# Half-filled experts added in pairs, the last sum read back early: a two-layer decoder trunk

## The chip, the cores and the metric

One core of a Trainium2 chip runs the whole program. The metric is the device time of one execution in microseconds (us). PE is TensorE, DVE is VectorE, ACT is ScalarE, POOL is GpSimd, and SP is SyncE, which issues nearly all weight transfers.

## The reference

512 tokens of width 1024 pass two layers. Each layer has a mixer and a mixture of experts, each shifted and scaled by six vectors that a product with `c` gives (adaLN), each followed by a layer norm.

```python
for layer in range(2):
    mod = silu(c) @ ada_w[layer] + ada_b[layer]
    sh1, sc1, g1, sh2, sc2, g2 = split(mod, 6)
    h = x * (1 + sc1) + sh1
    y = moba_gla_mixer(h, ...) if layer == 0 else gated_deltanet_mixer(h, ...)
    x = layer_norm(ALPHA * x + g1 * y)
    h = x * (1 + sc2) + sh2
    y = shared_expert(h) + sum over the token's 6 of 64 experts of
        weight * ((silu(h @ w_gate[e]) * (h @ w_up[e])) @ w_down[e])
    x = layer_norm(ALPHA * x + g2 * y)
```

All of it is float32. An expert has 3 MB of weights (gate and up 1024 x 256 each, down 256 x 1024).

## The kernel before

**Stages.** From 0 to 75 us the first modulation is made: eight slabs of `ada_w`, multiplied and summed by DVE (L256), turned by PE (L1743), applied to x in `start` (L1744 to L1751), and then the first projection starts. Layer 0's mixer runs to about 335 us, the routing to 402 us, its expert loop to 1028 us, layer 1's mixer and routing to 1496 us, and its expert loop to 2117 us; a tail with the last layer norm ends the program.

**Experts.** The experts are sorted by how many tokens chose them. The 20 fullest have a block of 128 slots of their own (called alone here), 28 share a block by two (twos, 14 blocks, 64 slots each), 16 by four (fours, 4 blocks, 32 slots each): 38 blocks for a layer, `BLOCKS`. The order in which the blocks run is made by `spread`. By experts in a block it is `11112121412121214121212121412121214122`.

**One turn of the loop** (`moe`, written out by hand, so the order on PE is that of the code). Turn b gathers the tokens of a later block (`xg`, an indirect DMA of POOL), turns them (`turn`, L1324), multiplies block b by gate and up (`widen`, L1336; ACT and DVE make `hh`), turns that back (`turn_back`, L1347), and multiplies block b-1 by down (`narrow`, L1369). A block of four has two experts at a time, so its `narrow` comes in two halves. What an alone block gives is added to a DRAM tensor `acc` by an indirect DMA of POOL (L1376). What a shared block gives is split in a high and a low part (`yh`, `yl`, L1383 to L1385) and goes to its tokens by matmuls with a 0/1 matrix (`combine`, L1396): for each of 8 tiles of 128 x 512 two matmuls, then one DVE add into x (L1397). The shared expert's down projection (`shared_end`, L1440) lies in turns 8 to 22.

**Weights.** SP issues them in order. Gate and up have five slots, down has a ring of three: the down weights of an expert can be issued when those of the third expert before have been used, and whatever stands behind them on SP waits too.

**End of the loop.** In the last turn POOL reads `acc` back in 8 pieces of 128 x 512 (L1615) and DVE adds them to x (L1616). Then all engines meet at a branch (`extra`, L1690, experts that outgrew their block: none here), the last block is added by L1396/L1397, and DVE does the layer norm (statistics L312 and L314, application L321 and L322; for x[0] in the last tail ACT and POOL, L329 to L331).

## Time and profile before

| | us |
|---|---|
| median of 3 runs (lowest to highest) | 2151.9 (2149.96 to 2156.48) |
| the profiled execution, its own time | 2150.13 |
| its span from first to last instruction | 2148.1 |
| PE busy | 1955.6 (91%) |
| DVE busy | 1236.2 (58%) |
| ACT busy | 508.3 (24%) |
| POOL busy | 441.2 (21%) |
| DMA queue of SP's transfers, share of 16 engines | 60.1% |

The shares are means over stages that differ: in the expert loops, 1247 of the 2148 us, PE and the DMA engines are both above nine tenths, elsewhere the DMA engines are far below.

### The profile page before, as it was taken

How to read it: one execution, taken by the hardware profiler on the slowest of the kernel's cores; microseconds unless marked ns; L12 is line 12 of the kernel's file. 1: busy time of each engine (PE TensorE's matmuls, PEld its weight loads, DVE VectorE, ACT ScalarE, POOL GpSimd, SP SyncE). 2: the span in 40 equal slices, each digit the busy share in tenths (PEclk: the TensorE clock that was granted, in tenths of full speed). 3: DMA queues.
4: the chain of work that ended last, by engine and by line, in shares of the span. 5: the costliest groups of instructions: out<-in, count | busy, mean ns of one | idle time of the engine just before them, and what ended most of it. 6: DMA issues, size and time to landing. Idle time of an engine off the chain costs nothing. (4 is left out here: it accounts for less than half of the span.)

```text
span 2148.1 us, 28655 instructions
## 1 busy us (share of the span) xinstructions
PE 1955.6 (91%) x10619; PEld 1193.5 (56%) x10619; DVE 1236.2 (58%) x3169; ACT 508.3 (24%) x969; POOL 441.2 (21%) x313
## 2 busy tenths in 40 slices
...
GB/s 296 257 240 186 182 199 195 352 330 325 406 349 351 389 316 361 381 325 300 96 118 59 40 60 60 46 99 309 357 335 365 363 327 402 353 317 405 329 348 126
DMA packets 128679, 572.18 MB, mean 266 GB/s; under 512 B 16943, under 2 KB 54255, under 8 KB 72473
## 3 DMA queue, kind: packets, MB, share of 16 engines
q1 hardware_dynamic: 103600, 499.81, 60.1%
...
q14 instruction: 58, 0.47, 0.1%
...
## 5 line engine op out<-in xcount | busy, mean ns | idle before, releaser
L1336 PE MATMUL ps_mm<-wslot,xT 128*64 128x512 f32 (+2 forms) x1216 | 404.5, 596 | 1.1 <-ACT xT L1325 0.8
L1369 PE MATMUL ps_mm<-wslot,hT 128*64 128x512 f32 (+2 forms) x1024 | 329.6, 627 | 20.1 <-DMA wslot<-in_moe_w_down_dram 19.9
L1338 DVE SCALAR_TENSOR_TENSOR hh<-hh,t,ps_mm 128x256 f32<-128x256 f32 x76 | 36.5, 480 | 434.5 <-ACT hh L1337 434.5
L1336 PE MATMUL ps_mm<-parts,xT 128*64 128x512 f32 (+2 forms) x832 | 280.0, 595 | 0.7 <-ACT xT L1325 0.4
L1336 PEld LDWEIGHTS ps_mm<-wslot,xT 128*64 128x64 f32 (+2 forms) x1216 | 142.1, 148 | 218.9 <-issue 205.7
L1369 PEld LDWEIGHTS ps_mm<-wslot,hT 128*64 128x64 f32 (+2 forms) x1024 | 105.5, 152 | 225.1 <-issue 197.5
L232 PE MATMUL ps_mm<-parts,hTh 128*128 128x256 f32 x704 | 206.7, 295 | 14.0 <-DVE op L400 6.9
L1294 POOL DMA_INDIRECT xg<-hd,idx x76 | 86.3, 1136 | 615.1 <-PE ps_tr L1396 525.4
L233 PE MATMUL ps_mm<-parts,hTh 128*128 128x256 f32 x704 | 204.0, 291 | 4.9 <-DVE parts L220 4.2
L234 PE MATMUL ps_mm<-parts,hTl 128*128 128x256 f32 x704 | 203.3, 291 | 0.0
L225 POOL TENSOR_TENSOR parts<-wslot,parts 128x512 fp32r<-128x512 f32 (+1 forms) x79 | 140.6, 1807 | 241.9 <-ACT parts L218 241.8
L1397 DVE TENSOR_TENSOR x<-x,ps_tr 128x512 f32<-128x512 f32 x288 | 183.6, 680 | 11.1 <-PE ps_tr L1396 10.4
L1337 ACT ACTIVATE hh<-ps_mm 128x256 f32<-128x256 f32 x76 | 29.2, 384 | 613.7 <-PE ps_mm L1336 613.7
L1376 POOL DMA_INDIRECT acc<-yh,row x40 | 64.8, 1620 | 498.9 <-DVE yh L1375 498.9
L1336 PEld LDWEIGHTS ps_mm<-parts,xT 128*64 128x64 f32 (+2 forms) x832 | 93.7, 144 | 130.5 <-issue 122.9
L1396 PE MATMUL ps_tr<-yh,ohs 128*128 128x512 f32 x288 | 137.4, 477 | 26.1 <-DVEq L1690 14.0
L232 PEld LDWEIGHTS ps_mm<-parts,hTh 128*128 128x128 f32 x704 | 137.3, 195 | 17.7 <-DVE op L400 4.6
L1325 ACT ACTIVATE xT<-ps_tr 128x512 f32<-128x512 f32 x152 | 84.0, 597 | 245.0 <-PE ps_tr L1324 245.0
L233 PEld LDWEIGHTS ps_mm<-parts,hTh 128*128 128x128 f32 x704 | 137.4, 195 | 6.8 <-DVE parts L220 4.8
L234 PEld LDWEIGHTS ps_mm<-parts,hTl 128*128 128x128 f32 x704 | 136.8, 195 | 2.2 <-issue 0.9
L234 PE MATMUL ps_mm<-hTh,parts 128*128 128x512 f32 (+1 forms) x296 | 120.6, 407 | 9.1 <-POOL parts L225 9.1
L232 PE MATMUL ps_mm<-hTh,parts 128*128 128x512 f32 (+1 forms) x296 | 123.7, 418 | 5.1 <-ACT parts L218 2.5
...
## 6 DMA issues: line engine op xcount, KB each, us to landing
wslot<-in_moe_w_down_dram SPq DMA_DIRECT2D x128, 1024.0 KB, 10.4
wslot<-in_moe_w_gate_dram SPq DMA_DIRECT2D x76, 1024.0 KB, 8.2
wslot<-in_moe_w_up_dram SPq DMA_DIRECT2D x76, 1024.0 KB, 11.7
parts<-in_moe_w_gate_dram SPq DMA_DIRECT2D x52, 1024.0 KB, 10.3
parts<-in_moe_w_up_dram SPq DMA_DIRECT2D x52, 1024.0 KB, 8.8
wslot<-in_ada_w_dram SPq DMA_DIRECT2D x44, 1024.0 KB, 5.6
wslot<-in_od_w_in_dram SPq DMA_DIRECT2D x16, 1024.0 KB, 6.2
wslot<-in_ev_w_in_dram SPq DMA_DIRECT2D x12, 1024.0 KB, 6.4
```

Of the source, the lines that this page charges most:

```text
L225: eng.tensor_sub(lo[:, ks], v[:, ks], hi[:, ks].bitcast(F32))
L232: self.nc.tensor.matmul(out, ah, bh, start=(i == 0), stop=False)
L233: self.nc.tensor.matmul(out, ah, bl, start=False, stop=False)
L234: self.nc.tensor.matmul(out, al, bh, start=False, stop=(i == n - 1))
L1294: self.nc.gpsimd.indirect_dma_start(out=xg, out_offset=None, in_=M["hd"], in_offset=bass.IndirectOffsetOnAxis(ap=idx, axis=0), bounds_chec ...
L1325: nc.scalar.activation(xT[:, 4 * g:4 * g + 4], pt.rearrange("p (k c) -> p k c", k=4), AF.Copy)
L1336: nc.tensor.matmul(pv[a:a + n], xT[:, i, a:a + n], w[0][:, :, i], start=(i == 0), stop=(i == KT - 1))
L1338: nc.vector.scalar_tensor_tensor(h, h, G["wt"], pg[:, FE:], op0=OP.mult, op1=OP.mult)
L1369: nc.tensor.matmul(py[a:a + n], hT[:, k, a:a + n], w[1][:, k, 512 * h:512 * h + 512], start=(k == 0), stop=(k == 1))
L1376: nc.gpsimd.indirect_dma_start(out=M["acc"], out_offset=bass.IndirectOffsetOnAxis(ap=G["tok"], axis=0), in_=yf, in_offset=None, bounds_che ...
L1396: nc.tensor.matmul(po, G["oh"][:, t], y[:, cs], start=(i + k == 0), stop=(i == len(Gs) - 1 and k == 1))
L1397: nc.vector.tensor_add(self.x[t][:, cs], self.x[t][:, cs], po)
```

## The change

The diff has these parts:

1. `width`: of an alone block's 128 slots only as many rows are scattered to `acc` as the expert's rank can need (128, 96 or 80: 2112 rows in a layer in place of 2560). `share` checks the smaller widths too, six small DVE instructions more in a layer.
2. `spread(..., 0.5, 3)`: another order of blocks, `11121214121211214121212112141212121422`; the last three are shared.
3. The result of an alone block has one buffer (`ys`), where it used two of `yh`; `hh` has one where it had two.
4. `combine` takes two blocks at a time: four matmuls fill one PSUM tile, and one DVE add takes it (the last blocks alone). The second half of a block of four's `narrow` goes to the end of the turn.
5. `acc` is read back in the third and second turn from the end, in 4 pieces of 128 x 1024 into the freed `xg` buffers, and POOL adds them to x.
6. In both tails the statistics of x[1] and x[3] are made by ACT (four instructions each); in the last tail half of x[1] is normalised by ACT and POOL, and the rows are stored in other pieces.
7. The eighth slab is issued ahead of the first projection's weights, and in `start` every second scaling of x runs on POOL.
8. In layer 0's last projection `fill(3, False)` lets the turning of the next modulation (L268, L269) come earlier.

```diff
+def width(k):
+
+    return P if k < SINGLE + 7 else 96 if k < SINGLE + 12 else 80
+
...
-    alone = [((k, 0, P),) for k in range(ALONE)]
+    alone = [((k, 0, width(k)),) for k in range(ALONE)]
     twos = shared(ALONE, TWOS, 2)
     fours = shared(ALONE + TWOS, E - ALONE - TWOS, 4)
-    return alone[:SINGLE] + spread(spread(twos, fours), alone[SINGLE:], 0, 1)
+    return alone[:SINGLE] + spread(spread(twos, fours), alone[SINGLE:], 0.5, 3)
...
+    def ln_stats_act(self, x, scratch):
+
+        nc = self.nc
+        mv = self.small.tile([P, 4], F32, tag="mv", name="mv", bufs=4)
+        sm = self.small.tile([P, 3], F32, tag="lnsum", name="lnsum", bufs=2)
+        nc.scalar.activation(scratch, x, AF.Copy, accum_out=sm[:, 0:1])
+        nc.scalar.activation(sm[:, 2:3], sm[:, 0:1], AF.Copy, scale=-1.0 / D)
+        nc.scalar.activation(mv[:, 0:1], sm[:, 0:1], AF.Copy, scale=1.0 / D)
+        nc.scalar.activation(scratch, x, AF.Square, bias=sm[:, 2:3], accum_out=sm[:, 1:2])
+        return mv, lambda: self.rsqrt(mv[:, 2:3], sm[:, 1:2], 1.0 / D, LN_EPS)
...
-        runs, k = [], ALONE
+        runs, k = [], SINGLE
+        for n in sorted({width(k) for k in range(SINGLE, ALONE)}, reverse=True):
+            m = sum(width(j) == n for j in range(SINGLE, ALONE))
+            if n < P:
+                runs.append((k, k + m))
+            k += m
...
-        one = G.get("one")
+        one = G.get("one", 0)
         if one:
-            (yh,) = [pool.tile([P, D], FR, tag="yh", name="yh", bufs=2)]
+            yf = pool.tile([P, D], F32, tag="ys", name="ys", bufs=1)
         elif "y" not in G:
...
-            yf = yh.bitcast(F32)
             for h, py in enumerate(pys):
                 cs = slice(512 * h, 512 * h + 512)
                 nc.vector.tensor_mul(yf[:, cs], py, M["grow"][:, cs])
-            nc.gpsimd.indirect_dma_start(out=M["acc"], out_offset=bass.IndirectOffsetOnAxis(ap=G["tok"], axis=0),
-                                         in_=yf, in_offset=None, bounds_check=S + P - 1, compute_op=OP.add)
+            nc.gpsimd.indirect_dma_start(out=M["acc"], out_offset=bass.IndirectOffsetOnAxis(ap=G["tok"][:one], axis=0),
+                                         in_=yf[:one], in_offset=None, bounds_check=S + P - 1, compute_op=OP.add)
             yield
             return
         for h, py in enumerate(pys):
...
+                    four = b > 0 and len(BLOCKS[b - 1]) > 2
+                    full = len(todo) == 2 or (todo and shared > nshared - 2)
+                    if not full and not four:
                         row.reverse()
                     for x in row:
                         next(x)
-                    for x in row:
+                    for x in row[four:]:
                         for _ in x:
                             pass
-                    if todo and b < NB:
-                        units = [lambda g=todo, t=t, h=h: self.combine(g, t, h) for t in range(TT) for h in range(2)]
+                    units, late = late, []
+                    if full and b < NB:
+                        late = [lambda g=todo, t=t, h=h: self.combine(g, t, h) for t in range(TT) for h in range(2)]
                         todo = []
+                        if not four:
+                            units, late = units + late, []
                     for u in units[:4]:
                         u()
                     if b + 1 < NB:
                         ahead()
-                    if b < NB and not units:
+                    if b < NB and not units and not four:
                         self.turn_back(M, G[b])
                     if b + 1 < NB:
                         self.turn(M, G[b + 1])
-                    if b < NB and units:
+                    if b < NB and (units or four):
                         self.turn_back(M, G[b])
                     next(sl, None)
                     for u in units[4:]:
                         u()
-                    units = []
...
-                    if b == NB - 1:
-                        for t in range(TT):
-                            for h in range(2):
-                                cs = slice(512 * h, 512 * h + 512)
-                                y = self.wk("acc")
-                                nc.gpsimd.dma_start(y, M["acc"][t * P:(t + 1) * P, cs])
-                                nc.vector.tensor_add(self.x[t][:, cs], self.x[t][:, cs], y)
+                    if NB - 3 <= b < NB:
+
+                        for t in back[b][0]:
+                            nc.gpsimd.tensor_add(self.x[t], self.x[t], M["xg"][(NB - 3 + t) % 3])
+                        for t in back[b][1]:
...
+                    for x in row[:four]:
+                        for _ in x:
+                            pass
...
             def stats(t):
-                M["mv"].append(self.ln_stats(self.x[t]))
-
-            mv = M["mv"]
+
+                if t % 2:
+                    m, then[t] = self.ln_stats_act(self.x[t], M["h"][t])
+                else:
+                    m = self.ln_stats(self.x[t])
+                mv.append(m)
...
+                sums(0)
+                stats(0)
                 if nxt:
-                    self.ln_next(self.x[3], mv[3], M["rows"], M["h"][3])
+                    sums(1)
+                    stats(1)
+                    norm(0)
+                    then[1]()
+                    sums(2)
+                    norm(1)
+                    stats(2)
+                    sums(3)
+                    stats(3)
+                    norm(2)
+                    then[3]()
+                    norm(3)
...
+                    self.ln_shift(mv[0])
+                    g0, g1 = norm2(0, slice(0, D)), norm2(1, lo)
+                    next(g0)
+                    next(g0)
+                    sums(1)
+                    stats(1)
+                    sums(2)
+                    stats(2)
+                    next(g0)
+                    next(g0)
+                    sums(3)
+                    stats(3)
+                    then[1]()
+                    self.ln_shift(mv[1])
+                    next(g1)
+                    norm(2)
+                    then[3]()
+                    for _ in g1:
+                        pass
+                    norm(1, hi)
+                    norm(3, lo)
+                    norm(3, hi)
...
-                    nc.vector.tensor_scalar(x, x, md[:, 1, k:k + 1], md[:, 0, k:k + 1], op0=OP.mult, op1=OP.add)
+                    eng = nc.gpsimd if k % 2 else nc.vector
+                    eng.tensor_scalar(x, x, md[:, 1, k:k + 1], md[:, 0, k:k + 1], op0=OP.mult, op1=OP.add)
...
-        for f in todo[:-2]:
+        for f in todo[:-1]:
             f()
         w_in = d["ev_w_in"][0]
         first = self.slab(w_in, 2048, 256)
-        todo[-2]()
         todo[-1]()
...
-            def fill(n=3):
+            def fill(n=3, wait=True):
...
-                    if i and len(queue) == 1:
+                    if wait and i and len(queue) == 1:
...
-            self.out_project(mixed, d["ev_w_out"][0], grow, d["x"][0], fill, (0, 1, 4, 5, 6, 7, 2, 3))
+            self.out_project(mixed, d["ev_w_out"][0], grow, d["x"][0], lambda: fill(3, False), (0, 1, 4, 5, 6, 7, 2, 3))
```

### The order on PE at the first block of four

Before, in layer 0. L1369 with 32x512 are the two halves of the four's `narrow`, L1336 is the next block's `widen`, L1396 adds the four's result, L1324 and L1347 turn; L1369 with 128x512 and 64x512 are the `narrow` of the alone block and of the block of twos that follow.

```order
L1369 MATMUL ps_mm<-wslot,hT 32x512 x8
L1336 MATMUL ps_mm<-wslot_4117,xT 128x512 x8
L1369 MATMUL ps_mm<-wslot,hT 32x512 x8
L1396 MATMUL ps_tr<-yh,ohs 128x512
L1396 MATMUL ps_tr<-yl,ohs 128x512
...
L1324 MATMUL ps_tr<-call,xg_2911 128x128 x8
L1347 MATMUL ps_sm<-call,hh 128x128 x2
...
L1336 MATMUL ps_mm<-wslot_4128,xT 64x512
...
L1369 MATMUL ps_mm<-wslot,hT 128x512 x4
...
L1369 MATMUL ps_mm<-wslot,hT 64x512 x8
```

Now (the lines moved: L1390 is `narrow`, L1357 `widen`, L1416 the adding, L1345 and L1368 the turning, L1460 `shared_end`):

```order
L1390 MATMUL ps_mm<-wslot,hT 32x512 x8
L1357 MATMUL ps_mm<-parts,xT 128x512 x8
L1345 MATMUL ps_tr<-call,xg_2910 128x128 x8
L1368 MATMUL ps_sm<-call,hh 128x128 x2
...
L1460 MATMUL ps_mm<-wd,sh 128x512 x2
L1390 MATMUL ps_mm<-wslot,hT 32x512 x8
L1357 MATMUL ps_mm<-wslot_4029,xT 64x512
...
L1390 MATMUL ps_mm<-wslot,hT 128x512 x4
...
L1390 MATMUL ps_mm<-wslot,hT 64x512 x8
L1357 MATMUL ps_mm<-wslot_4117,xT 128x512 x8
L1416 MATMUL ps_tr<-yh,ohs 128x512
```

The second half moved from ahead of the adding and turning to the end of the turn, and the 16 matmuls that add the four's result no longer stand between it and the `narrow` of the next block of twos: they come with that block's own.

### The order on PE where a shared block's result is added

Before, the first block of twos in layer 0; the numbers tell the buffers apart (`ps_tr` is the PSUM tile that one DVE add empties):

```order
L1396 MATMUL ps_tr_4029<-yh_3992,ohs_3994 128x512
L1396 MATMUL ps_tr_4029<-yl_3993,ohs_3994 128x512
L1396 MATMUL ps_tr_4033<-yh_3992,ohs_3994 128x512
L1396 MATMUL ps_tr_4033<-yl_3993,ohs_3994 128x512
L1396 MATMUL ps_tr_4037<-yh_3992,ohs_3994 128x512
L1396 MATMUL ps_tr_4037<-yl_3993,ohs_3994 128x512
```

Now, the first pair:

```order
L1416 MATMUL ps_tr_4157<-yh_3911,ohs_3913 128x512
L1416 MATMUL ps_tr_4157<-yl_3912,ohs_3913 128x512
L1416 MATMUL ps_tr_4157<-yh_4120,ohs_4122 128x512
L1416 MATMUL ps_tr_4157<-yl_4121,ohs_4122 128x512
L1416 MATMUL ps_tr_4163<-yh_3911,ohs_3913 128x512
L1416 MATMUL ps_tr_4163<-yl_3912,ohs_3913 128x512
L1416 MATMUL ps_tr_4163<-yh_4120,ohs_4122 128x512
L1416 MATMUL ps_tr_4163<-yl_4121,ohs_4122 128x512
```

A tile was full after two matmuls, and is now full after four, of two blocks; the number of matmuls is the same.

### The order on POOL at the end of layer 1's loop

Before: gathers (L1294), scatters (L1376), and then the eight readings of `acc`.

```order
L1376 DMA acc_12151<-yh,row 640x1024
L1294 DMA xg_12116<-hd_11944,idx 128x1024
L1294 DMA xg_12117<-hd_11944,idx 128x1024
L1376 DMA acc_12151<-yh,row 640x1024 x2
L1615 DMA acc<-acc_12151 128x512 x8
```

Now, L1396 the scatter, L1642 the reading, L1640 the adding:

```order
L1396 DMA acc_12015<-ys,row 640x1024
L1642 DMA xg_11982<-acc_12015 128x1024
L1642 DMA xg_11980<-acc_12015 128x1024
L1640 TENSOR_TENSOR x<-x,xg_11982 128x1024
L1642 DMA xg_11982<-acc_12015 128x1024
L1640 TENSOR_TENSOR x<-x,xg_11980 128x1024
L1642 DMA xg_11981<-acc_12015 128x1024
L1640 TENSOR_TENSOR x<-x,xg_11981 128x1024
L1640 TENSOR_TENSOR x<-x,xg_11982 128x1024
```

The additions moved from DVE, where they stood behind the last `narrow`'s work, to POOL, and the readings stand two turns earlier. On SP the eighth slab (L252, 128x2048) and the first projection's weights (L206, 128x8x256) changed places.

## Rows read from the trace of the kernel before

**Rows 1.** Windows, expert loop: length, busy us (x) PE..POOL, PEclk, DMA share, GB/s.

```profile
402.00:1028.00 626.00, 602.42 (x2476) 270.10 (x2475) 289.22 (x853) 81.92 (x153) 71.50 (x60) 0.98 0.92 348
```

**Rows 2.** Waits of PE, 430 to 1020: total us, times, longest.

```profile
PE ps_mm L1369 <- DMA wslot<-in_moe_w_down_dram: 9.6, 4, 3.5
...
PE ps_tr L1396 <- DVE yl L1385: 3.8, 4, 1.0
```

**Rows 3.** Waits of PE, 1470 to 2110.

```profile
PE ps_mm L1369 <- DMA wslot<-in_moe_w_down_dram: 10.3, 4, 4.2
```

**Rows 4.** Timeline of PE, first block of four: start, length, instruction [idle before].

```profile
535.37 7.13 PE L1336 MATMUL ps_mm<-wslot,xT 128*128 128x512 f32 x16
...
544.88 3.62 PE L1369 MATMUL ps_mm<-wslot,hT 128*32 128x512 f32 x14 [1.40 <-DMA wslot<-in_moe_w_down_dram]
...
562.60 3.70 PE L1369 MATMUL ps_mm<-wslot,hT 128*128 128x512 f32 x8
...
569.36 3.65 PE L1369 MATMUL ps_mm<-wslot,hT 128*64 128x512 f32 x16
```

**Rows 5.** Timeline of PE, one block of twos added to x.

```profile
579.51 0.80 PE L1396 MATMUL ps_tr<-yh,ohs 128*128 128x512 f32 x1
...
580.38 0.40 PE L1396 MATMUL ps_tr<-yh,ohs 128*128 128x512 f32 x1
...
581.07 0.40 PE L1396 MATMUL ps_tr<-yl,ohs 128*128 128x512 f32 x1
...
582.26 1.31 PE L1324 MATMUL ps_tr<-call,xg 128*128 128x128 f32 x8
...
583.75 0.48 PE L1396 MATMUL ps_tr<-yh,ohs 128*128 128x512 f32 x1
...
585.89 0.64 PE L1336 MATMUL ps_mm<-parts,xT 128*64 128x512 f32 x1
```

**Rows 6.** DMA issues from 549.0 to 549.2: count, KB, us to landing.

```profile
wslot<-in_moe_w_up_dram SPq DMA_DIRECT2D x1, 1024.0 KB, 17.5
```

**Rows 7.** Waits of PE, 1020 to 1080.

```profile
PE ps_tr L1396 <- DVEq L1690: 8.0, 1, 8.0
```

**Rows 8.** Waits of PE, 2110 to 2149.

```profile
PE ps_tr L1396 <- DVEq L1690: 6.0, 1, 6.0
```

**Rows 9.** Timeline behind the last down projection of layer 0.

```profile
1027.57 3.09 DVE L1616 TENSOR_TENSOR x<-x,acc 128x512 f32<-128x512 f32 x5
...
1034.29 0.68 DVE L1383 TENSOR_TENSOR y<-ps_mm,grow 128x512 f32<-128x512 f32 x1
...
1036.01 0.79 PE L1396 MATMUL ps_tr<-yh,ohs 128*128 128x512 f32 x1 [7.98 <-DVEq L1690]
```

**Rows 10.** Groups of VectorE, 2117 to 2148: count, busy us, mean ns, idle before.

```profile
L1397 DVE TENSOR_TENSOR x<-x,ps_tr 128x512 f32<-128x512 f32 x8 | 5.2, 680 | 0.3 <-PE ps_tr L1396 0.3
...
L312 DVE BATCH_NORM_STATS2 bn<-x 128x6 f32<-128x512 f32 x8 | 5.1, 682 | 0.0
...
L322 DVE SCALAR_TENSOR_TENSOR x<-x,mv,wd 128x512 f32<-128x512 f32 x2 | 1.5, 752 | 0.1
```

**Rows 11.** Groups of GpSimd, the whole span.

```profile
L330 POOL TENSOR_TENSOR x<-x,wd 128x1024 f32<-128x1024 f32 x1 | 2.4, 2377 | 1.5 <-ACT x L329 1.5
...
L1458 POOL TENSOR_TENSOR h<-h,lnrow 128x1024 f32<-128x1024 f32 x2 | 6.5, 3258 | 0.2
```

**Rows 12.** Timeline of the start.

```profile
35.73 2.29 DVE L220 TENSOR_TENSOR parts<-wslot,parts 128x2048 fp32r<-128x2048 f32 x1 [3.82 <-ACT parts L218]
...
37.94 2.35 DVE L256 SCALAR_TENSOR_TENSOR acc<-wslot,cact,acc 128x2048 f32<-128x2048 f32 x1
...
40.43 3.36 PE L1743 MATMUL ps_tr<-call,acc 128*128 128x128 f32 x16 [7.66 <-DVE acc L256]
...
43.55 0.47 PE L232 MATMUL ps_sm<-hTh,parts 128*16 128x512 f32 x1
```

**Rows 13.** Waits of PE, 75 to 430.

```profile
PE ps_tr L268 <- DVE mod L269: 4.1, 1, 4.1
```

44 lines of the change are left out of this document (24 added, 20 removed).

## The prediction

> **What bounds it now.** I read the windows first, one for each stage. In the expert loop of layer 0 PE is busy 602.4 of 626.0 us while the DMA engines move data 0.92 of the time [rows 1]; layer 1's loop is alike. So a loop ends when PE ends, and PE waits only where weights or results are late. Next I read who lets PE wait there. Four waits for down weights (9.6 us in layer 0, 10.3 in layer 1) and four for `yl` (3.8) head the list [rows 2, 3]. The timeline puts them in one place: the second half of a block of four starts with 1.40 us of idle time because its down weights have not landed [rows 4], and the adding right behind it waits for `yl`. A list of waits misses what is only slow: in the adding, the first eight matmuls of a block take from 579.51 to 582.26, the other eight from 583.75 to 585.89, 4.9 us together, while three steps between 580.38 and 581.07 show 0.23 us for a matmul that nothing holds [rows 5]. DVE's add, one for two matmuls, takes 0.68 [rows 10], so PE is paced by DVE there. Behind each loop PE stands still at the branch, 8.0 and 6.0 us [rows 7, 8], and then DVE's layer norm is the chain to the end.
>
> **The adding in pairs.** With four matmuls for each DVE add PE needs 4 x 0.23 = 0.92 us for a tile and DVE 0.68, so PE sets the pace: two blocks take 32 x 0.23 = 7.4 us where they took 2 x 4.9 = 9.8. Eight pairs give 8 x 2.4 = 19 us per layer. If PE kept the pace of the better half (2.14 / 8 = 0.27), two blocks would take 8.6 and the gain would be 10. Nothing in a row makes the four-matmul tile wait, so I take 18. The `yl` waits go because the four's result is added a turn later: 3.5 of 3.8.
>
> **The late half of `narrow`.** It now starts later by a turning (the timeline's 1.31 us is the most for it, 582.26 to 583.41) and small work, about 1.7 us, at the first two fours by `shared_end` as well, some 1.9 more. Against waits of 1.4 to 3.5 us that leaves about 2.8 of 9.6: a gain of 6.8, between 4 and 9.6.
>
> What is late next is the point. SP's queue holds all following loads behind the slot that this half frees. Before, the half ended at 548.5 (544.88 + 3.62), and the next block of twos needed its down weights at 569.36 [rows 4], 20.9 us later, the four's adding lying in between. Now only a `widen` (7.13), an alone `narrow` (3.70) and 1.7 of turning do, 12.5 us. The last weights issued ahead of those down weights, at 549.1, needed 17.5 us to land [rows 6], until 566.6, which is 18.1 us behind the half's end. The half itself ends up to 2.2 us later than before (1.7 + 1.9 - 1.4), and most of the loads ahead don't wait for it. So three of the four fours (the third is followed by two alone blocks) get a new wait of 3.5 to 5.7 us at the `narrow` of the next twos. I take 4.5, a cost of 13.5 per layer, with 0 (the queue drains earlier, since 448 of 2560 scattered rows are gone) and 8 each as the ends.
>
> Per layer: -18 -3.5 -6.8 +13.5 = -14.8; two layers -29.6. Layer 1's rows differ by 0.7 us, so I count it alike. The new order of blocks itself moves only where these stalls stand; single `ys` and `hh` buffers are covered by the 12 us or more of PE work between two uses.
>
> **The two tails.** In the tail of layer 0, PE's last matmul ended 7.98 us before 1036.01, at 1028.0. DVE was in the L1616 adds (3.09 us for five from 1027.57) and made the last `y` only at 1034.29; PE went on 1.04 us after that [rows 9]. Without those adds `y` follows the last matmul by 0.68, so the wait is about 1.7: a gain of 6.3, and 4.3 of the 6.0 in layer 1. POOL's adds of x[2] and x[3] lie behind the adding of the turn before, which ends 3.65 us ahead of the last matmul's end: 2 x 2.38 [rows 11] makes about 1.1 us beyond it, under the 1.7. Those 2.38 are for 128 x 1024, two inputs. The same shape took 3.26 in another line (L1458), where DVE ran an instruction with two SBUF inputs beside it; then the adds end 2.9 behind the matmul, and the gain is 1.2 smaller in each tail. The adds here run beside DVE adds that read PSUM, as L330 did, so I keep 2.38 and take off 0.6 in each tail for the doubt. The Trainium skill, "GPSIMD Engine Reference", Key points, says that GpSimd shares its SBUF interfaces with VectorE and contends with VectorE instructions in a two-port mode or with two SBUF inputs. By that rule POOL's adds, beside DVE adds that take one input from PSUM, would not be slowed, and without my 0.6 in each tail the forecast would be 2102; the half of x[1] that is normalised on GpSimd in the last tail, beside L321 and L322, would be. The two rows above agree with it.
>
> The layer norm's chain on DVE loses, for two of four tiles, two L312 of 0.68 and one L314 of 0.21, 3.1 us in each tail [rows 10]; ScalarE's passes over 1024 columns (bounded by POOL's 2.38) lie beside the next tile's adds. In the last tail half of x[1] (L321 and L322, 2 x 0.75) leaves too. I take 2.3 of 3.1 in the first tail, since PE and ScalarE's copies stand there as well, and 3.3 of 4.6 in the last. Together -(6.3 - 0.6 + 2.3) = -8 and -(4.3 - 0.6 + 3.3) = -7; ends -4 and -9.5, -3 and -9.
>
> **Start, projection, ahead of the loops.** The eighth slab's sum at 37.94 stood behind the 2.29 us of L220 at 35.73, which had itself waited 3.82; the turning began at 40.43 and the first projection matmul at 43.55 [rows 12]. With the slab first, its sum can follow the seventh's, some 5 us earlier, but the projection's weights then land later and their low part (L220) comes behind the reductions. I take -3.5, ends 0 and -5.4. L268 waited 4.1 us for L269 [rows 13]; made earlier, while DVE sat idle, most of it goes: -3, ends 0 and -4.1. The six more DVE instructions and the later shared-expert products ahead of each loop cost about 1 us each: +2, ends 0 and +4.
>
> **Sum.** -29.6 - 8 - 7 - 3.5 - 3 + 2 = -49.1 on the profiled 2150.1 gives 2101.0. The median of the runs is 1.8 above that execution, so I forecast 2103.
>
> **Rivals.** (1) *The loads take back what the loops gain.* The DMA engines are at 0.92 and a shorter loop asks for more. With new waits of 8 us at six places and the adding at 0.27: per layer -10 -3.5 -6.8 +24 = +3.7, in all +7.4 - 19.5 = -12.1, that is 2140. For it: the 17.5 us landing of a load of 1 MB [rows 6]. Against it: 0.08 of 626 us, 50 us, are free. (2) *The tails give nothing*, because the meeting at the branch waits for POOL's adds or for the readings of `acc`, and ScalarE's statistics come too late for the norm: -15 becomes 0, 2118. For it: POOL issues in order, so a reading stands behind the add of x[0]. Against it: readings start two turns, over 20 us, ahead. (3) *Slower*: SP's queue, held at the down slot until the turn's end, lets the next twos wait long. The loops lose where six waits of w outweigh all else, -76.1 + 6w > 6.5: w above 13.8. At 15 it is 2166. The longest landing here, 17.5, would have to count from the half's end plus 9 us. (4) *No difference*, between these.
>
> **How the numbers follow.** Runs here spread by 0.3%, so 0.3% (6.5 us) tells from no change. Forecast 0.62, rival 1 0.18, rival 2 0.12, rival 3 0.04, rival 4 0.04. The forecast's own range, from its bounds, is 2086 to 2118. The range that holds 8 in 10 reaches into rival 1, 2084 to 2136. Faster 0.92 (forecast, rivals 1 and 2), same 0.04, slower 0.04.
>
> **What would show it.** Loops: waits for down weights move from the second halves of fours to the `narrow` of twos two blocks on (three in a layer, 3 to 6 us each), `yl` waits are gone, 32 adding matmuls take about 7.5 us, the loop takes 605 to 617 us in place of 626. Branch: PE waits 1.5 to 3 us. Start: the first projection matmul at about 40. Wrong would be waits of 8 us and more behind the fours, an adding that keeps 0.3 us a matmul, or a PE that waits at the branch for POOL.

## The result, and the profile after

| | before | after |
|---|---|---|
| median of the runs, us (lowest to highest) | 2150.93 (2146.26 to 2156.48) | 2172.01 (2170.12 to 2173.84) |
| span of the profiled execution | 2148.1 | 2168.2 |

The ratio is 1.0097 (95% interval 1.0071 to 1.0123). The change makes the kernel 21 us slower, where 49 us faster was forecast. By stages of the two spans:

| stretch | before | after | difference | forecast |
|---|---|---|---|---|
| up to the first `widen` of layer 0 | 402.5 | 395.6 | -6.9 | -5.5 |
| expert loop, layer 0 | 625.5 | 641.5 | +16.0 | -14.8 |
| from there to the first `widen` of layer 1 | 468.2 | 465.2 | -3.0 | -7 |
| expert loop, layer 1 | 620.8 | 634.2 | +13.4 | -14.8 |
| last tail | 31.1 | 31.8 | +0.7 | -7 |

(The pre-loop +2 of the forecast is put half into the first row, half into the third.) So the loops lost 59 us against the forecast and the tails 12; the first stretch came out 1.4 us better. Each row compares one execution with one: in the 18 kernels of this document that have the changed start, the first stretch took 393.3 to 399.9 us, so a difference of a few us in one stretch says little. The windows of the two loops of the changed kernel, in the columns of [rows 1]:

```profile
395.60:1037.10 641.50, 599.06 (x2470) 281.06 (x2470) 255.72 (x781) 79.56 (x152) 85.12 (x63) 0.97 0.88 337
1502.30:2136.50 634.20, 594.76 (x2470) 279.90 (x2470) 254.11 (x780) 77.75 (x151) 85.31 (x63) 0.97 0.89 340
```

VectorE has 33 us less to do in a loop than in [rows 1], where PE had waited 3.8 us for its `yl` [rows 2] and had been paced by it in the adding. TensorE's busy time is nearly what it was, its clock is lower, and the DMA engines move nearly the same bytes in a longer time. The waits of PE in the loop of layer 0, then of layer 1, answer to [rows 2, 3]:

```profile
PE ps_mm L1390 <- DMA wslot<-in_moe_w_down_dram: 29.9, 7, 9.1
...
PE ps_mm L1390 <- DMA wslot<-in_moe_w_down_dram: 27.9, 6, 9.3
```

Waits for down weights went from 9.6 to 29.9 us and from 10.3 to 27.9; those for `yl` are gone, as forecast. The timeline of PE behind the first block of four, the place of [rows 4], shows the first long one:

```profile
530.72 1.45 PE L1390 MATMUL ps_mm<-wslot,hT 128*32 128x512 f32 x4
532.10 7.09 PE L1357 MATMUL ps_mm<-wslot,xT 128*64 128x512 f32 x32
539.12 3.70 PE L1390 MATMUL ps_mm<-wslot,hT 128*128 128x512 f32 x8
...
545.67 1.04 PE L1390 MATMUL ps_mm<-wslot,hT 128*64 128x512 f32 x2 [1.65 <-DMA wslot<-in_moe_w_down_dram]
555.84 5.80 PE L1390 MATMUL ps_mm<-wslot,hT 128*64 128x512 f32 x14 [9.13 <-DMA wslot<-in_moe_w_down_dram]
```

PE is ready for the `narrow` of the next twos at 544.0 (545.67 less 1.65), 11.9 us behind the end of the four's late half (530.72 + 1.45); 12.5 was forecast. The second expert's down weights were issued by SP at 533.30; the view of DMA issues from 533.2 to 533.4 has the time to their landing, 22.5 us, as its last column:

```profile
wslot<-in_moe_w_down_dram SPq DMA_DIRECT2D x1, 1024.0 KB, 22.5
```

They landed at 555.8, 23.6 us behind the half's end, where 18.1 was forecast. The windows around it:

```profile
535.00:545.60 10.60, 9.02 (x42) 4.04 (x38) 3.60 (x14) 1.47 (x3) 1.62 (x1) 1.00 1.01 418
545.60:550.00 4.40, 1.04 (x2) 0.19 (x2) 0.00 (x0) 0.00 (x0) 1.03 (x1) 0.99 1.02 385
550.00:560.20 10.20, 4.36 (x12) 1.28 (x13) 0.65 (x1) 0.00 (x0) 0.00 (x0) 0.50 1.02 386
560.20:570.00 9.80, 9.80 (x29) 4.62 (x26) 2.95 (x6) 1.64 (x3) 0.00 (x0) 1.00 0.95 390
```

The DMA engines are full all along (1.01 to 1.04 in every 5 us from 515 to 565), so the load stood behind bytes that had been issued before it. It was itself issued 1.1 us after the late half's end, and from 510 to 515, with SP waiting for buffers, the DMA engines had been busy for only 0.29: what an earlier issue would have gained is not shown here. The granted clock falls to 0.50 (1.2 GHz) from 550.0 to 560.2: it fell 3 us into the wait and stayed low 4 us beyond it, so the first matmuls behind the wait ran at half pace (14 in 5.80 us; the same tile took 3.65 for 16 in [rows 4]). Summed over the loops, TensorE had 1.2 GHz for 27.3 and 13.7 us before, and 44.4 and 41.0 after; leaving out what lies in waits, it worked at that clock for 23.9 and 13.7 us before, 32.3 and 24.9 after. If work at 1.2 GHz takes twice its time, half of the difference is lost, which is an estimate: 4.2 and 5.6 us. With the longer waits (+20.3 and +17.6) that makes 24.5 and 23.2 us. The adding gives back 14.9 and 17.5 (below); the 6 and 8 us that are left to the +16.0 and +13.4 are spread over the loop in pieces that I did not trace one by one.

One pair's adding (L1416), with what stands behind each half of it:

```profile
568.13 0.79 PE L1416 MATMUL ps_tr<-yh,ohs 128*128 128x512 f32 x1
...
572.19 1.06 PE L1345 MATMUL ps_tr<-call,xg 128*128 128x128 f32 x8
...
573.53 0.47 PE L1416 MATMUL ps_tr<-yh,ohs 128*128 128x512 f32 x1
...
577.28 1.88 PE L1460 MATMUL ps_mm<-wd,sh 128*128 128x512 f32 x4
```

The other waits of layer 0's loop stand here:

```profile
710.82 5.11 PE L1390 MATMUL ps_mm<-wslot,hT 128*64 128x512 f32 x14 [7.81 <-DMA wslot<-in_moe_w_down_dram]
...
863.94 5.32 PE L1390 MATMUL ps_mm<-wslot,hT 128*32 128x512 f32 x14 [2.99 <-DMA wslot<-in_moe_w_down_dram]
...
1001.77 1.94 PE L1390 MATMUL ps_mm<-wslot,hT 128*64 128x512 f32 x2 [6.50 <-DMA wslot<-in_moe_w_down_dram]
1004.67 6.22 PE L1390 MATMUL ps_mm<-wslot,hT 128*64 128x512 f32 x13 [0.95 <-DMA wslot<-in_moe_w_down_dram]
```

128*64 is a block of twos, 128*32 a block of four. So the long waits are at twos: behind the first four (1.65 and 9.13), behind the second (7.81), and at the end of the loop, where the fourth four is followed by twos at once (6.50 and 0.95). The third and fourth four wait at their own second half (2.99, and 0.88 at 991.65). In layer 1 it is 8.78, 9.29 and 7.43 at the twos, 0.94 and 1.44 at fours. The code says why the first two fours differ: each comes first in its pair and is held until the next twos are done, while the third and fourth find a block of twos waiting and are added in the turn that follows.

In the tail of layer 0 (timeline, VectorE and GpSimd around the last `narrow`; compare [rows 9]):

```profile
1033.45 4.67 POOL L1640 TENSOR_TENSOR x<-x,xg 128x1024 f32<-128x1024 f32 x2 [30.80 <-DVE x L1417]
...
1034.47 3.93 DVE L1407 TENSOR_SCALAR ohs<-call,t 128x128 fp32r<-128x128 f32 x3
...
1038.33 0.68 DVE L1403 TENSOR_TENSOR y<-ps_mm,grow 128x512 f32<-128x512 f32 x1
...
1042.14 0.79 PE L1416 MATMUL ps_tr<-yh,ohs 128*128 128x512 f32 x1 [5.00 <-DVEq L1761]
```

Three one-hot rows (L1407), each 0.27 us when alone, take 3.93 on VectorE while GpSimd's two additions run, and `y` stands behind them. The view from 1036 to 1037 shows the second of each:

```profile
1035.78 2.34 POOL L1640 TENSOR_TENSOR x<-x,xg 128x1024 f32<-128x1024 f32 x1
1035.82 2.39 DVE L1407 TENSOR_SCALAR ohs<-call,t 128x128 fp32r<-128x128 f32 x1
```

It ends 0.09 us behind the addition (1038.21 and 1038.12), and so did the first (1.42 us, to 1035.90, the addition to 1035.81); the third, behind both, took 0.28. So a one-hot row that began beside an addition ended only when that did. The wait at the branch is 5.0 us, where 1.7 was forecast and 8.0 was before. In the last tail the same pair of neighbours appears once more: VectorE's first two L337/L338 of 128x512 beside GpSimd's L1691 take 1.75 and 1.56, the next two 0.74 and 0.75:

```profile
2159.59 3.20 POOL L1691 TENSOR_TENSOR x<-x,wd 128x512 f32<-128x512 f32 x2
2159.91 1.75 DVE L337 SCALAR_TENSOR_TENSOR x<-x,mv,wd 128x512 f32<-128x512 f32 x1
2161.77 1.56 DVE L338 SCALAR_TENSOR_TENSOR x<-x,mv,wd 128x512 f32<-128x512 f32 x1
2163.26 0.74 DVE L337 SCALAR_TENSOR_TENSOR x<-x,mv,wd 128x512 f32<-128x512 f32 x1
2164.03 0.75 DVE L338 SCALAR_TENSOR_TENSOR x<-x,mv,wd 128x512 f32<-128x512 f32 x1
```

The first projection matmul is at 38.06 in place of 43.55 [rows 12], with VectorE's low part now behind the reductions:

```profile
36.71 0.69 DVE L1815 TENSOR_REDUCE md<-ps_tr 128x4 f32<-128x512 f32 x1
...
37.33 2.29 DVE L225 TENSOR_TENSOR parts<-wslot,parts 128x2048 fp32r<-128x2048 f32 x1
38.06 0.62 PE L237 MATMUL ps_mm<-parts,hTh 128*128 128x256 f32 x3
```

This lead did not last. The same matmul of the first projection stands at 75.36 before and at 75.16 after:

```profile
75.36 0.47 PE L234 MATMUL ps_mm<-parts,hTl 128*128 128x256 f32 x1
...
75.16 0.28 PE L239 MATMUL ps_mm<-parts,hTl 128*128 128x256 f32 x1
```

What makes the first stretch shorter comes behind it. PE's waits between 75 us and the loop, one line of before and two of after:

```profile
PE ps_mm L234 <- POOL parts L225: 6.6, 3, 3.0
...
PE ps_mm L237 <- ACT hTh L367: 5.2, 1, 5.2
...
PE ps_mm L239 <- POOL parts L230: 1.6, 1, 1.6
```

The waits for GpSimd's low parts fell by 5.0 us, for which the prediction has no term. The 4.1 us for L268 [rows 13] are gone, but a wait of 5.2 us for ScalarE (`hTh`) stands at the next product: around it, from 328 to 366 us, the lead does not grow (8.4 and 8.1 us).

### The profile page after: what moved, and what is told of

It is laid out like the page before. It is cut to its first block, busy times and chain, and to the rows that moved or that the text cites. A ratio compares the mean times of both kernels' runs of the same rounds, so it can differ in the third digit from the quotient of the medians.

```text
span 2168.2 us, 28525 instructions
## 1 busy us (share of the span) xinstructions
PE 1952.4 (90%) x10619; PEld 1216.7 (56%) x10619; DVE 1161.9 (54%) x3022; ACT 514.8 (24%) x994; POOL 467.6 (22%) x319
## 5 line engine op out<-in xcount | busy, mean ns | idle before, releaser
L1357 PE MATMUL ps_mm<-wslot,xT 128*64 128x512 f32 (+2 forms) x1216 | 408.8, 603 | 3.5 <-ACT xT L1346 2.5
L1390 PE MATMUL ps_mm<-wslot,hT 128*64 128x512 f32 (+2 forms) x1024 | 338.0, 632 | 58.0 <-DMA wslot<-in_moe_w_down_dram 57.8
L1357 PE MATMUL ps_mm<-parts,xT 128*64 128x512 f32 (+2 forms) x832 | 301.4, 603 | 1.1 <-ACT xT L1346 0.9
L1357 PEld LDWEIGHTS ps_mm<-wslot,xT 128*64 128x64 f32 (+2 forms) x1216 | 144.3, 148 | 210.9 <-issue 200.0
L1390 PEld LDWEIGHTS ps_mm<-wslot,hT 128*64 128x64 f32 (+2 forms) x1024 | 107.8, 153 | 267.0 <-issue 203.5
L237 PE MATMUL ps_mm<-parts,hTh 128*128 128x256 f32 x704 | 208.2, 297 | 13.7 <-DVE op L416 9.0
L1315 POOL DMA_INDIRECT xg<-hd,idx x76 | 93.0, 1224 | 527.7 <-PE ps_tr L1416 230.1
L1396 POOL DMA_INDIRECT acc<-ys,row x40 | 61.6, 1541 | 536.6 <-DVE ys L1395 536.6
L1357 PEld LDWEIGHTS ps_mm<-parts,xT 128*64 128x64 f32 (+2 forms) x832 | 102.6, 149 | 131.6 <-issue 121.6
L237 PEld LDWEIGHTS ps_mm<-parts,hTh 128*128 128x128 f32 x704 | 137.9, 196 | 17.6 <-ACT parts L223 6.7
L1416 PE MATMUL ps_tr<-yh,ohs 128*128 128x512 f32 x288 | 127.0, 442 | 19.3 <-DVEq L1761 10.0
L261 DVE SCALAR_TENSOR_TENSOR acc<-wslot,cact,acc 128x2048 f32<-128x2048 f32 x38 | 117.9, 3103 | 11.7 <-DMA wslot<-in_ada_w_dram 11.3
## 6 DMA issues: line engine op xcount, KB each, us to landing
wslot<-in_moe_w_down_dram SPq DMA_DIRECT2D x128, 1024.0 KB, 11.1
wslot<-in_moe_w_up_dram SPq DMA_DIRECT2D x76, 1024.0 KB, 10.4
```

The source lines that it names most:

```text
L237: self.nc.tensor.matmul(out, ah, bh, start=(i == 0), stop=False)
L261: nc.vector.scalar_tensor_tensor(acc, w, self.cact[:, k:k + 1], acc, op0=OP.mult, op1=OP.add)
L1315: self.nc.gpsimd.indirect_dma_start(out=xg, out_offset=None, in_=M["hd"], in_offset=bass.IndirectOffsetOnAxis(ap=idx, axis=0), bounds_chec ...
L1357: nc.tensor.matmul(pv[a:a + n], xT[:, i, a:a + n], w[0][:, :, i], start=(i == 0), stop=(i == KT - 1))
L1390: nc.tensor.matmul(py[a:a + n], hT[:, k, a:a + n], w[1][:, k, 512 * h:512 * h + 512], start=(k == 0), stop=(k == 1))
L1396: nc.gpsimd.indirect_dma_start(out=M["acc"], out_offset=bass.IndirectOffsetOnAxis(ap=G["tok"][:one], axis=0), in_=yf[:one], in_offset=None ...
```

## The experiments

Each kernel differs from the changed one, or from a mixed one named with it, in the lines shown. "Loops" are the two expert loops, "waits" PE's waits of over 0.4 us for loads in each of them, "1.2 GHz" the time at the low clock in each, all of the profiled execution. Each ratio is to the kernel before, which ran beside each group of them (2148.5 to 2150.9 us).

| kernel | median us | ratio (95%) | loops | waits | 1.2 GHz |
|---|---|---|---|---|---|
| before | 2150.9 | 1 | 625.5, 620.8 | 9.6, 10.3 | 27, 14 |
| after | 2172.0 | 1.0097 (1.0071 to 1.0123) | 641.5, 634.2 | 29.9, 27.9 | 44, 41 |
| `half_back` | 2164.7 | 1.0077 (1.0053 to 1.0101) | 635.1, 634.0 | 23.3, 22.8 | 38, 38 |
| `wide` | 2156.2 | 1.0029 (1.0016 to 1.0043) | 635.4, 632.7 | 26.9, 26.7 | 38, 34 |
| `adds_dve` | 2162.5 | 1.0057 (1.0039 to 1.0075) | 637.0, 637.9 | 26.3, 29.5 | 44, 44 |
| `wide_adds` | 2157.9 | 1.0039 (1.0021 to 1.0058) | 634.4, 634.5 | 26.9, 26.4 | 38, 41 |
| `before_light` | 2142.9 | 0.9972 (0.9953 to 0.9992) | 605.7, - | 1.4, - | 3, - |
| `after_light` | 2117.9 | 0.9851 (0.9834 to 0.9867) | 596.8, - | 0, - | 17, - |
| `unpaired` | 2167.1 | 1.0085 (1.0066 to 1.0105) | 637.1, 636.3 | 17.4, 15.7 | 34, 34 |
| `old_loop` | 2148.8 | 0.9999 (0.9986 to 1.0013) | 630.9, 626.3 | 16.6, 15.7 | 24, 14 |
| `old_loop_late_read` | 2130.7 | 0.9903 (0.9874 to 0.9933) | 620.9, 616.3 | 11.3, 9.3 | 14, 10 |
| `pairs_old_order` | 2130.4 | 0.9898 (0.9857 to 0.9939) | 616.6, 616.6 | 19.9, 19.0 | 17, 21 |
| `late_half_alone` | 2147.7 | 0.9987 (0.9966 to 1.0008) | 625.0, 622.9 | 13.7, 13.6 | 17, 17 |
| `dve_stats` | 2130.7 | 0.9906 (0.9875 to 0.9937) | 620.9, 615.0 | 11.1, 10.9 | 14, 3 |
| `new_order_late_read` | 2167.5 | 1.0097 (1.0073 to 1.0121) | 634.3, 634.0 | 14.4, 14.6 | 31, 31 |
| `end_422_late_read` | 2149.4 | 1.0011 (0.9997 to 1.0024) | 627.7, 626.3 | 14.9, 12.4 | 17, 24 |
| `pairs_fours_alone` | 2105.4 | 0.9801 (0.9777 to 0.9825) | 604.2, 606.6 | 8.1, 7.5 | 10, 21 |
| `add_after_branch` | 2132.9 | 0.9934 (0.9910 to 0.9959) | 620.0, 615.6 | 11.4, 11.1 | 10, 3 |
| `after_fours_at_once` | 2143.5 | 0.9976 (0.9958 to 0.9994) | 624.8, 620.2 | 16.2, 14.8 | 27, 24 |
| `full_scatter` | 2113.6 | 0.9835 (0.9813 to 0.9856) | 609.0, 612.0 | 10.4, 12.1 | 14, 24 |

### The late half, another order, and the tail's additions

`half_back` puts the four's second half back ahead of the turning:

```diff
-                    for x in row[four:]:
+                    for x in row:
...
-                    for x in row[:four]:
-                        for _ in x:
-                            pass
```

> The changed kernel with one thing undone: the second half of a four's down projection runs directly behind the next block's widen again, as before the change. The changed kernel waits 29.9 and 27.9 us for down weights in its two loops, 9.1, 7.8 and 7.4 of them in layer 0 at the twos two blocks behind a four. Theory 1 (too little PE work lies between a four and the next twos, whatever the half does): the half starts about 3.5 us earlier where shared_end lies in between and waits 2 to 3.5 us at each four again, the waits at the twos shrink by 2 to 4 each; loops the same within 5 us each, in all 2165 to 2175. Theory 2 (the half, moved late, holds SP's queue, and that alone made the new waits): the waits at the twos fall below 2 us, each loop becomes 12 to 18 us shorter, in all 2136 to 2150.

`wide` keeps everything but the order of the blocks, with two alone blocks behind three of the fours:

```diff
-    return alone[:SINGLE] + spread(spread(twos, fours), alone[SINGLE:], 0.5, 3)
+    kinds = {1: iter(alone), 2: iter(twos), 4: iter(fours)}
+    return [next(kinds[int(c)]) for c in "11121214112212141122121411221214111222"]
```

> The changed kernel with another order of blocks: behind each four stand two blocks of one expert before the next twos (1112 12, then three times 1411 2212, then 1411 1222); the late half stays. Theory 1 (too little PE work between a four and the next twos): a further widen and narrow, 10.8 us, lie in between, the waits of 7 to 9 us at the twos go to 0 to 2, and with them most of the stretches at 1.2 GHz (44 and 41 us in the changed kernel); each loop 20 to 30 us shorter, in all 2112 to 2134. Theory 3 (PE is now too fast for the loads anywhere): about as much waiting shows up at other blocks, each loop within 8 us, in all 2156 to 2175. Theory 2 (the late half holds SP's queue) expects waits to stay behind each four at another block, 2160 or more.

`adds_dve` gives the additions of x[2] and x[3], the two that stand beside the last `narrow`, to VectorE; `wide_adds` is both.

```diff
-                            nc.gpsimd.tensor_add(self.x[t], self.x[t], M["xg"][(NB - 3 + t) % 3])
+                            eng = nc.vector if t > 1 else nc.gpsimd
+                            eng.tensor_add(self.x[t], self.x[t], M["xg"][(NB - 3 + t) % 3])
```

> The changed kernel with the additions of x[2] and x[3] from the DRAM sum on VectorE, those of x[0] and x[1] stay on GpSimd. In the changed kernel three VectorE instructions that make the 0/1 matrix (L1407, 0.23 us each) take 3.9 us at the end of each loop, while GpSimd's two additions (4.67 us) run, and PE waits 5.0 us at the branch. Theory A (GpSimd's two-input additions hold up VectorE's fast-mode instructions): L1407 takes under 1 us there, PE waits 2 to 3.5 us, each tail 1.5 to 3 us shorter, in all 3 to 6 us less, 2166 to 2169. Theory B (those instructions waited for something else, such as the last down projection): the wait stays at 5 us or grows by the 2.6 us that two additions on VectorE take, 2172 to 2177.

> The order of blocks with two single blocks behind each four, and the additions of x[2] and x[3] on VectorE, together. If theories 1 and A hold and the two are independent: the gains add, 2107 to 2131. If theory 3 and B hold: 2156 to 2178.

Putting the half back gives 7 us, in layer 0's loop alone: waits of 1.3 to 3.3 us come back at the fours, and 2.9 and 5.5 remain at the twos behind the first two, so the result lies between the two theories. Another order gives 16, but only 6 and 1.5 of them in the loops: now all four fours are held, each has its wait at the next twos (7.9, 5.1, 6.9 and 3.6 in layer 0), and the waits stay 27 us long; the rest comes from the stretch between the loops and the tail. As to the additions, on VectorE they take 2.35 us together, the one-hot rows are short again, and the wait at the branch falls from 5.0 to 2.2 us. Timeline of VectorE in `adds_dve`, then PE's wait at the branch:

```profile
1034.28 2.35 DVE L1641 TENSOR_TENSOR x<-x,xg 128x1024 f32<-128x1024 f32 x2
1036.55 1.28 DVE L1403 TENSOR_TENSOR y<-ps_mm,grow 128x512 f32<-128x512 f32 x2
1037.75 0.28 DVE L1407 TENSOR_SCALAR ohs<-call,t 128x128 fp32r<-128x128 f32 x1
...
PE ps_tr L1416 <- DVEq L1762: 2.2, 1, 2.2
```

The last tail is 28.2 us long in place of 31.8. On top of `wide` the same edit gains nothing (2157.9 to 2156.2): there a VectorE product of 2.28 us stands ahead of the additions, and the wait at layer 0's branch stays long (5.1 us, 4.7 without the edit).

### Are the loads what takes the gain back?

`before_light` and `after_light` load only half of each expert's weights and multiply with that half twice, so their output is another; layer 1's routing changes with it, and only layer 0 is compared.

```diff
-        self.nc.sync.dma_start(v, src.rearrange("(p k) c -> p k c", p=P))
+        k = v.shape[1] // 2
+        self.nc.sync.dma_start(v[:, :k], src.rearrange("(p k) c -> p k c", p=P)[:, :k])
```

> The kernel before with half of the expert weights: each load brings half of its bytes, and the matmuls read the loaded half twice, so PE's instructions stay as many and as long; the output is another. Beside the changed kernel with half of the weights it shows the loops when loads don't bind. Theory L (around the fours the loops run at the rate of the loads): the four waits for down weights (9.6 and 10.3 us) and most of the low clock (27 and 14 us) go, each loop 12 to 22 us shorter, in all 2110 to 2128.

> The changed kernel with half of the expert weights in the same way. Theory L (the new waits are a matter of the loads' rate; the adding in pairs does save PE about 10 us a loop and more): waits for down weights fall from 30 and 28 us to under 4, low clock from 44 and 41 us to under 20, the loops fall to 590 to 602 and are 8 to 18 us shorter than those of the light kernel before, in all 2078 to 2098. Rival R (single buffers, the late half or the order of blocks cost PE time of themselves): loops as long as those of the light kernel before or longer, 2110 and more.

With the loads out of the way the changed loop is 8.9 us shorter than that before (596.8 to 605.7), with them 16.0 longer. So some 25 us of the loop depend on how the order of PE's work meets the loads. The changed loop still has 17 us at 1.2 GHz here in place of 3, without a wait for loads.

### Pairs or order?

`unpaired` is the changed kernel with every shared block added alone, and the half back; `old_loop` also has the order of the kernel before up to its last four blocks (it must end with three shared blocks, since the sums are read two turns early) and VectorE's additions.

```diff
-                    full = len(todo) == 2 or (todo and shared > nshared - 2)
+                    full = bool(todo)
```

```diff
+    return [next(kinds[int(c)]) for c in "11112121412121214121212121412121211422"]
```

> The changed kernel with each shared block added by itself again (two matmuls for a DVE add) and the late half put back behind the widen; order of blocks, readings and tails as changed. Undoing the late half alone gave 2164.7 against 2149.9 of before. Theory P (the pairs bunch the loads: two blocks of twos run without the adding between them, then twice the adding, while a load lands every 2.5 us): waits for down weights 9 to 15 us a loop, low clock below 30, loops 622 to 630, in all 2138 to 2152. Theory O (the order of blocks makes the waits): they stay above 20 us a loop, 2160 or more.

> As the run before, and also the order of blocks before the change (with its last single block moved ahead of the last four, so that the early reading of the DRAM sum still comes behind the last scatter), and the additions of x[2] and x[3] on VectorE. What is left of the change: start, layer 0's projection, narrower scatters, early readings, ScalarE's statistics. Theory P: waits as before (8 to 12 us a loop), loops 620 to 627, start 7 us earlier, tails 2 to 6 us shorter in all, 2132 to 2142. Theory O expects it 10 us or more below the run before this one; theory P within 8 us of it.

Without any pairs the loops still take 637 and 636 us: at that point I held the order for the cause, and the pairs for neutral. The next kernels start from `old_loop_late_read`: the whole order of before, each block added alone, the half back, `acc` read in the last turn with VectorE's additions; start, widths, single buffers, early turning and the layer norms are the change's.

```diff
-                    if NB - 3 <= b < NB:
...
+                    if b == NB - 1:
+                        for t in range(TT):
+                            for h in range(2):
+                                cs = slice(512 * h, 512 * h + 512)
+                                y = self.wk("acc")
+                                nc.gpsimd.dma_start(y, M["acc"][t * P:(t + 1) * P, cs])
+                                nc.vector.tensor_add(self.x[t][:, cs], self.x[t][:, cs], y)
```

> The loop of before (its order of blocks, each shared block added by itself, the half directly behind the widen, the DRAM sum read in the last turn and added on VectorE) with the start, layer 0's projection, the narrower scatters and the tails of the change. If the loss lies in the loop alone, the loops are 621 to 627 us again and the start keeps its 7 us: 2138 to 2146. If the narrower scatters or the single buffers cost, loops of 630 and more, 2150 or more.

`pairs_old_order` adds the change's pairs to it (`full` as in the change), `late_half_alone` only the late half, `dve_stats` makes all statistics on VectorE.

> As the run before, with the adding in pairs. Theory P (pairs bunch the loads): the adding takes 10 to 15 us less, waits for down weights grow from about 10 to 18 to 25 us and low clock to 30 and more; loops 620 to 632, within 6 us of the run without pairs in all. If pairs are worth what they save on PE: loops 605 to 615, 2115 to 2126.

> As the first of these runs (no pairs, order of before), with the second half of a four's narrow at the end of the turn. If the late half only moves the stall: the four waits of 1.4 to 4.2 us become less than 1.5 us each, and new ones of 3 to 8 us stand at the next twos; loops 3 us shorter to 8 us longer. If it is worth its own: loops 5 to 9 us shorter, waits below 4 us a loop.

> As the first of these runs, with the statistics of x[1] and x[3] on VectorE again. In the changed kernel ScalarE's statistics of x[3] lie in the last tail between 2153.5 and 2158.3 and VectorE waits for them. If ScalarE's statistics are what made the last tail 31.8 us long in place of 24: the tails become 1 to 4 us shorter. If they save what two VectorE statistics cost (3.1 us a tail): 2 to 6 us longer in all.

The mixture `old_loop_late_read` beats the kernel before by 1%. Its loops are 4.6 and 4.5 us shorter than that kernel's, which is what the narrower scatters turn out to be worth (below). The late half costs 4.1 and 6.6 us of the loops here (17 of the median): it moves the waits from the fours to the twos behind them and makes them longer. ScalarE's statistics are worth nothing that can be seen. The pairs cut the time from one adding matmul's start to the next instruction's by 15 us in a loop (83.3 to 68.3), and the loops shorten by 4 and 0: waits grow by 9 and 10. The long ones of `pairs_old_order` (6.4 and 5.5, then 4.5 and 7.0) again stand at the twos behind the first two fours, the two that are held in this order too.

### Which part of the order?

`new_order_late_read` and `end_422_late_read` are `old_loop_late_read` with the order of the change, and with that of `old_loop` (whose end alone differs from before).

> The first mixed kernel (the one that beat both, with its sums read back in the last turn, each shared block added alone, the narrow product in one piece) with only the block order of the changed kernel put in place of that of the kernel before. Theory O (the order itself costs the loop its time, through longer load waits and the slow clock behind them): loops 634 to 639 us instead of 621 and 616, load waits 15 to 19 us, 1.2 GHz for 30 us or more in each loop, time 2158 to 2172. Theory R (the early reading of the sums, which the new order allows, is what costs; the order by itself little): loops 617 to 625 us, time 2128 to 2142. Between the two (626 to 633 us) both have a share.

> The same mixed kernel with the order of the kernel before except at its end, where three shared blocks (four, two, two experts) stand last instead of one. Theory E (the three shared blocks at the end are what the loop pays for, since their loads of 4 to 8 MB come where no block of one expert lies between): loops 627 to 633 us, a load wait of 5 us or more in the last 35 us of the loop, time 2140 to 2152. Theory R (the early reading): loops 619 to 624 and 615 to 620 us, time 2129 to 2138.

The three shared blocks at the end cost 6.8 and 10.0 us, the rest of the order another 6.6 and 7.7. The wait of 5 us that theory E asked for at the end did not come, only 2.8 and 4.7 at the last twos. Reading the sums early costs little by itself (`old_loop` against `end_422_late_read`: +3.2 and 0.0).

### Held fours

`add_after_branch` is told below. `pairs_fours_alone` is `pairs_old_order` with one condition more. As it ran, a four is never held for a later partner; where a two already waits, the four is added together with it.

```diff
-                    full = len(todo) == 2 or (todo and shared > nshared - 2)
+                    full = len(todo) == 2 or (todo and shared > nshared - 2) or (todo and four)
```

> The mixed kernel that adds in pairs, but a block of four is never a second of a pair and is added as soon as it is done; only twos are held for a partner. If the long waits at the twos come from two shared blocks' worth of adding that is left out and then done at once in front of a four's loads (theory P), the load waits fall from 19 to 20 us to 11 to 15 us per loop, loops 608 to 614 us, time 2115 to 2125. If what the adding saves on TensorE is taken back wherever the loads are short (theory L), load waits stay within 3 us of what the saving in adding (some 9 instead of 14 us) leaves: loops 615 to 620 us, time 2126 to 2136.

It is the fastest kernel of all, 43 us under the kernel before on the same chip, at 0.980: what the pairs save now arrives (loops 17 and 10 us shorter than `old_loop_late_read`). Its windows:

```profile
396.00:1000.20 604.20, 587.28 (x2474) 284.90 (x2474) 257.17 (x791) 79.31 (x152) 77.53 (x60) 0.99 0.92 357
...
1465.70:2072.40 606.70, 591.06 (x2474) 285.63 (x2474) 257.24 (x794) 77.53 (x151) 79.21 (x63) 0.98 0.92 354
```

`after_fours_at_once` is the same line in the changed kernel itself, and nothing else.

> The changed kernel with one line more: a block of four is never held for a partner; it is added in the turn behind its own, with a two if one waits. Nothing else differs. Theory H (holding a four takes 5 us of TensorE's work out of the place where its 8 loads are still short, and the long waits at the next twos and the slow clock behind them come from that): the waits of 9.1, 7.8, 8.8 and 9.3 us fall to 1 to 4 us, 1.2 GHz from 44 and 41 us to 20 to 32 us, loops 620 to 628 us, time 2140 to 2155. Theory O' (in the new order the loads are short anyway, since the same block runs with 17 us more per loop also without pairs): the waits fall by less than 5 us in a loop, loops 632 to 640, time 2160 to 2175.

One line takes 28 us off the changed kernel: loops -16.7 and -14.0, waits -13.7 and -13.1, and 17 us less at 1.2 GHz in each loop (10 and 6 of them working time). It also shifts which blocks pair up behind the first four: the second four now finds a block of twos waiting. Its timeline at the place of the first long wait (its loop begins 2.2 us later) shows why:

```profile
539.64 3.70 PE L1390 MATMUL ps_mm<-wslot,hT 128*128 128x512 f32 x8
542.77 0.80 PE L1416 MATMUL ps_tr<-yh,ohs 128*128 128x512 f32 x1
...
548.62 0.39 PE L1416 MATMUL ps_tr<-yl,ohs 128*128 128x512 f32 x1
548.86 7.03 PE L1357 MATMUL ps_mm<-wslot,xT 128*128 128x512 f32 x16
555.81 4.15 PE L1390 MATMUL ps_mm<-wslot,hT 128*64 128x512 f32 x16
```

The four's adding (6.1 us with the turning in it) stands ahead of the twos' `narrow`. And these twos, now the first of a pair, have their `narrow` behind the next `widen` (7.0 us): the code puts it ahead only in a turn that completes a pair, as it must be done before the adding. So their `narrow` comes at 555.81 without a wait; in the changed kernel PE was there at 544.0, and the last of the weights came at 555.8. The two effects were not tried apart. A wait remains at the next twos, which complete the pair, 5.6 us long, and one of 6.5 at the end of the order.

With these runs the loops' +16.0 and +13.4 can be followed in four measured steps (each could be worth something else in another sequence):

| step | loop, layer 0 | loop, layer 1 |
|---|---|---|
| from before to `old_loop_late_read` (narrower scatters, single buffers) | -4.6 | -4.5 |
| to `new_order_late_read` (the order of blocks) | +13.4 | +17.7 |
| to `after_fours_at_once` (pairs, late half, early reading) | -9.5 | -13.8 |
| to the changed kernel (a four is held for a partner) | +16.7 | +14.0 |

### What else is in it

`full_scatter` is `pairs_fours_alone` with all 128 rows of each alone block scattered.

```diff
-    return P if k < SINGLE + 7 else 96 if k < SINGLE + 12 else 80
+    return P
```

> The kernel that holds only twos for a partner, with all 128 slots of each alone block scattered to the sum in DRAM as before (2560 rows of 4 KB in a layer in place of 2112). If that traffic takes room from the weights' loads: load waits 2 to 5 us longer in each loop, loops 607 to 612 us, time 2111 to 2119. If it does not matter beside some 200 MB of weights in a loop: loops within 2 us of 604 and 607, time 2101 to 2109, perhaps 1 us less for the six small VectorE instructions ahead of each loop that go with the widths.

The narrower scatters, 448 rows of 4 KB in a layer, are worth some 8 us of the time, 5 in each loop. The two ratios differ by 0.34% and their intervals overlap by 0.1%, but the loops of `old_loop_late_read` say the same. `add_after_branch` is `old_loop_late_read` with the additions of x[0] to x[2] on VectorE behind the branch and that of x[3] on GpSimd.

```diff
-                                nc.vector.tensor_add(self.x[t][:, cs], self.x[t][:, cs], y)
...
+                if t < 3:
+                    nc.vector.tensor_add(self.x[t], self.x[t], sums_of[t])
```

> The mixed kernel, with the sums of the blocks of one expert read into the freed buffers of gathered tokens in the last turn, and added to the residual on VectorE behind the branch for token tiles 0 to 2 and on GpSimd for tile 3. Theory A (the branch waits because VectorE's making of the last one-hot rows stands behind the eight additions and GpSimd's work): the wait of the first adding behind the branch falls from 7.9 and 5.9 to 2 to 3 us, the tail of layer 0 is 4 to 6 us shorter, the last tail 31.0 becomes 27 to 30 us since VectorE has three more 128x1024 additions there, time 2122 to 2128. Rival (the additions only move from ahead of the branch to behind it on VectorE, which is the engine that the tail waits for): no change, 2128 to 2134.

The rival holds in the time: the wait of the first adding behind the branch falls from 7.9 and 5.9 us to 3.4 and 2.3, but the last tail is 33.4 us long in place of 31.0.

## Why the prediction was wrong

What failed is the prediction of the loops, -14.8 each, in two steps. The order of blocks was put at nothing and cost 13.4 and 17.7 us. The wait behind the fours was put at +13.5 and, with what a held four takes along, cost about what the pairs gave. Both were tried by themselves: not holding the fours (`after_fours_at_once`) brings 17 and 14 us, the old order in place of the new one, without pairs (`old_loop_late_read` against `new_order_late_read`), 13 and 18.

- **The new wait (+13.5 per loop).** The sign was right, and the number of long waits, three in a loop. Their size was not: 26.0 us in layer 0 (1.65 + 9.13, 7.81, 6.50 + 0.95) and 25.5 in layer 1. PE came when it was forecast to; the landing of 17.5 us that I took from one row [rows 6] was 22.5 for the load in question. "The queue drains earlier" was my good end; from 515 to 565 the DMA engines were full, so PE's coming earlier turned into waiting. The places were right for the first two fours only. No four in this order is followed by two alone blocks, as I wrote of the third: the third is not held and has no wait behind it, and the fourth is followed by twos at once.
- **Holding the four.** The text named the four's adding as what had lain in between, but not that the third four keeps it there, being added in the turn that follows, and not that a completed pair also pulls the twos' `narrow` ahead of the `widen`. The one-line experiment puts this step at 17 and 14 us per loop, nearly what the pairs were to save.
- **"The new order of blocks itself moves only where these stalls stand."** This failed: measured without pairs, the order costs 13.4 and 17.7 us per loop (621 and 616 to 634), half of it or more by its end with three shared blocks. The wait of 7.4 us at the loop's end goes with the order: it stays, 6.5 and 0.95, when the fours are not held. I did not count the loads' bytes against PE's work block by block, which might have shown it.
- **The clock.** The sum had nothing for TensorE's clock. By the estimate above it cost 4.2 and 5.6 us per loop, most of it behind the long waits.
- **The adding (-18).** Right in the mechanism: a pair's 32 matmuls took 7.8 us, 16 from 568.13 to 572.19 and 16 from 573.53 to 577.28, where 7.4 was forecast (lines above). Over the loop, from each adding matmul's start to the next instruction's, it is 86.8 to 71.9 and 86.4 to 68.9, so -15 and -17.5.
- **The late half (-6.8).** It lost, 4.1 and 6.6 us, where it was tried alone. In the changed kernel 3.9 and 2.4 us of waits stayed at the fours, where 2.8 was forecast, so the term itself was near; what it lost came back at the twos.
- **The tails (-8 and -7).** They gave -3.0 and +0.7. The 0.6 us of doubt for GpSimd's additions was too small, and looked at the wrong victim: the additions kept their pace (4.67 for two, 2.38 each forecast [rows 11]), and VectorE's one-hot rows were held for 3.1 us (3.93 less 3 x 0.27). The rule cited in the prediction (the Trainium skill, "GPSIMD Engine Reference", Key points) speaks of contention with VectorE instructions in a two-port mode or with two SBUF inputs; I applied it to VectorE's PSUM additions and to the last tail's half of x[1], not to the one-hot rows. The PSUM additions kept their 0.68 us beside GpSimd, and L337 and L338, with two SBUF inputs, went from 0.75 to 1.75 and 1.56, so there the trace agrees. Whether L1407 runs in a two-port mode no run here shows; that two of three were held until GpSimd's addition ended, the trace does. The statistics on ScalarE, forecast at 2.3 and a part of 3.3, gave nothing that can be seen (`dve_stats`).
- **Start and L268 (-6.5).** The first stretch came out 6.9 us shorter, but by luck. The first projection matmul was 5.5 us earlier, and none of that was left at 75 us; L268's wait [rows 13] went, and another of 5.2 us took its place; 5.0 us came from waits for GpSimd that no term names.
- **The range.** The ends given for the single terms, added up, reach from about 2060 to 2162; for the narrower 2086 to 2118 the prediction shows no sum. The measured 2172 lies outside both.

Rival 3 held in its outcome, but not in its price: it asked for six waits of 13.8 us, and the loss came from six of 8.6 on average with costs beside them that no case had. Of its mechanism, SP held at the down slot by the late half, `half_back` shows 6.4 and 0.2 us of the loops; the rest of the loss stays without it. What stays open: of the order's cost (13.4 and 17.7 us) the waits are 3.1 and 5.3, and half of 16.8 and 18.3 us more work at 1.2 GHz makes 8.4 and 9.2; that is worked out from the traces, and nothing was tried on the clock by itself. Of the 20.6 and 13.6 us between `after_fours_at_once` and `pairs_fours_alone` the shares of the order, the late half and the early reading were not taken one by one.
